# Sixteen of 62 SBUF slots begin 64 bytes later, and a planner's rule says which tiles take them

## The chip, the cores and the metric

The kernel runs on one core of a Trainium2 chip. The metric is the time of one execution on the device in microseconds (us), median of several runs.

## The reference

Two layers on a sequence of 512 tokens with 1024 features, all in float32. Each layer has a token mixer (retention in layer 0, mLSTM in layer 1) and a feed-forward part with a causal convolution. Both mixers have four heads with 256-wide queries and keys and 512-wide values. Without norms, gates and conditioning:

```
q, k, v, g = split(h @ w_in)
s   = (q @ k.T) * decay          # per head; in the mLSTM exp-weights instead of decay
y   = s @ v                      # causal, per head
x   = x + gate * ((silu(g) * norm(y)) @ w_out)
u   = conv(h2 @ w_up);  a, b = split(u)
x   = x + gate2 * ((silu(a) * b) @ w_down)
```

## The kernel before, in words

**Numbers as pairs.** Every operand of a large product is split into a high and a low part in the single-pass matmul type (names end in `h` and `l`, or are `whi` and `wlo`), and a product takes three matmuls: high by high, high by low, low by high (`mm3`, line 659). In each matmul a stationary operand, 128 by 128, is loaded by a weight load (PEld), and a moving operand of 256, 384 or 512 columns streams past it. Most weight products are folded: seven half-width products in place of eight (`PairStream`, `ValueStream`, line 781), with 256 columns each.

**Where tiles lie.** Activations lie in 62 equal slots of 128 partitions by 2048 bytes (`slot`, line 412, `NSLOTS`), weights in 18 wide tiles of 4352 bytes (`wide`, line 415). In the built program every slot begins at the same place modulo 128 bytes, and so does every wide tile. A folded weight begins `OFF` = 16 words, 64 bytes, into its wide tile (lines 552 to 640); so do the weights of the half-width contractions (`boundary`, line 1077), one block in a tile of the down projection (`Beside.low`, line 540) and the constant `ones_d`. Weights used at the full width of 512 columns have no offset.

**Attention.** `scores` (line 1293) multiplies a stretch of keys (stationary) with queries (moving) in four strips of 512, 384, 256 and 256 columns, into bank `psc`; `attend` (line 1320) multiplies values (stationary) with the weights of the scores `sh`, `sl` (moving) in the same strips, into bank `pav`. All four operands lie in slots. The pairs of values are made by `center_split` and `plain_split` (lines 1002, 1013), the keys by `rope` (line 1552, layer 0, name `qk`) and `conv_then` (layer 1, name `mqk`). Between heads stand two small products with a constant `ones_v` or `ones_1`, 512 wide: `pvar`, `pmu`, `pden`.

**The order of the work.** The kernel is first recorded as a list of calls. `Plan.run` (line 268) then plays a list scheduler over it with cost estimates and due times, and issues each engine's instructions in the order that it finds. A tile gets its slot there, when its first writer is placed: `room` holds for each kind the free slots with the time at which they come free, and the one that has been free longest is taken:

```
if b.bufs:
    b.at = room[b.key].pop(0)[1]
```

The real tile is made at issue (`Buf.get`, line 101), with a tag made of the kind and the slot number; its first writer waits for the readers of the slot's last tenant. All instructions are issued through line 387 of the kernel, so the profile's rows have that line, and names tell them apart.

Of the kernel before, what the change touches and what calls it, by code (L numbers as in the profile page):

```python
# [10 lines left out]
F32 = mybir.dt.float32  # L11
F32R = mybir.dt.float32r
# [4 lines left out]
P = 128  # L17
T = 512
# [19 lines left out]
LEAD = (4.0, 4.5)  # L38
WPAD = 64
OFF = 16  # L40
DIRECT = (0, 0)
ROOT_AT = 1
SPLIT = 4
# [3 lines left out]
NSLOTS = 62  # L47
# [46 lines left out]
class Buf:  # L94


    def __init__(self, pool, shape, dt, tag, name, bufs, psum=False):
        self.args, self.shape, self.key, self.bufs, self.psum = (pool, shape, dt, tag, name), shape, tag, bufs, psum
        self.real, self.uses, self.log, self.at = None, 0, [], ""

    def get(self):
        if self.real is None:
            pool, shape, dt, tag, name = self.args
            self.real = pool.tile(shape, dt, tag=f"{tag}{self.at}", name=name)
        return self.real

# [46 lines left out]
class Plan:  # L153
# [114 lines left out]
    def run(self):  # L268
# [38 lines left out]
        def choose(e):  # L307
# [17 lines left out]
            t, n = min((t, n) for _, n, t in cand if t > soonest)  # L325
            return t, e, n

        best = {e: choose(e) for e in engines}
        while len(out) < len(calls):
            if not any(best.values()):  # L330
# [8 lines left out]
            for b in c.bufs:  # L339
                if b.log is not None:  # L340
                    b.log, b.busy = None, 0.0
                    if b.bufs:
                        b.at = room[b.key].pop(0)[1]
                        dirty.update(engines)
                        makers[b.key].remove(b.maker)
            occ = c.occ
# [23 lines left out]
            for m, real in c.succs:  # L370
                s = calls[m]
# [19 lines left out]
def trunk(ctx: ExitStack, tc: tile.TileContext, xT, cb, pos, vec, ident, decay, zmask, ada, w_s0, w_in0, w_v0,  # L391
          w_o0, w_in1, w_v1, w_f1, w_o1, w_up, w_dn, out):
    nc = tc.nc
    const = ctx.enter_context(tc.tile_pool(name="const", bufs=1))
    slots = ctx.enter_context(tc.tile_pool(name="slots", bufs=1))
    wpool = ctx.enter_context(tc.tile_pool(name="wpool", bufs=1))
    asides = ctx.enter_context(tc.tile_pool(name="asides", bufs=1))
    cond = ctx.enter_context(tc.tile_pool(name="cond", bufs=1))
# [6 lines left out]
    def uid(s):  # L405
        count[0] += 1
        return f"{s}_{count[0]}"

    def tile_of(pool, shape, dt, tag, name):
        return Buf(pool, shape, dt, tag, name, KINDS.get(tag, 0), tag == "ps")  # L410

    def slot(s, dt=F32, w=T):
        return tile_of(slots, [P, w], dt, "s", uid(s))

    def wide(s, dt=F32):
        return tile_of(wpool, [P, WCOLS + WPAD], dt, "w", uid(s))
# [7 lines left out]
    def fixed(pool, shape, dt, name):  # L424
        b = tile_of(pool, shape, dt, name, name)
        b.get()
        return b
# [5 lines left out]


    V.memset(fixed(const, [P, 32], F32, "pad")[:], 0.0)
    ones = {}
    for name, v in (("d", 1.0 / D), ("v", 1.0 / DV), ("1", 1.0)):
        off = OFF if name == "d" else 0
# [78 lines left out]
    class Chunk:  # L517
        def __init__(self, src, n, off, added=False):
            self.off, self.added = off, added
            self.raw = wide("raw")[:, off : off + n]  # L520
            S.dma_start(self.raw, src)
# [122 lines left out]
                self.p[name] = hi, low_by(name in VADDED)(raw[r], hi, OFF)  # L644

    class Pair:
        def __init__(self, s, w=T):
            self.hi, self.lo = slot(s + "h", F32R, w), slot(s + "l", F32R, w)

        def split(self, src, r=slice(None), eng=None):  # L650
            A.copy(self.hi[:, r], src)
            (eng or V).tensor_tensor(self.lo[:, r], src, self.hi[:, r].bitcast(F32), op=ALU.subtract)

    def pair_of(s, src):
        p = Pair(s)
        p.split(src)
        return p

# [343 lines left out]
    def center_split(v, ps):  # L1002

        t, m = slot("vt"), tile_of(cols, [P, 1], F32, "vm", uid("vm"))
        tf = t[:]
        A.activation(tf, ps[:], AF.Copy, accum_out=m[:])
        G.tensor_scalar(m[:], m[:], -1.0 / DV, None, op0=ALU.mult)
        p = Pair("v")
        A.activation(p.hi[:], tf, AF.Identity, bias=m[:])
        V.scalar_tensor_tensor(p.lo[:], tf, m[:], p.hi[:].bitcast(F32), op0=ALU.add, op1=ALU.subtract)  # L1010
        v.append(p)

    def plain_split(v, ps):
        p = Pair("v")
        p.split(ps[:])
        v.append(p)

# [531 lines left out]
        A.activation(k[:], k[:], AF.Square)  # L1549
        G.tensor_scalar(cos[:], k[:], -2.0, 1.0, op0=ALU.mult, op1=ALU.add)  # L1550

    def rope(p1, p2):
        t = [slot("rp")[:] for _ in range(4)]
        V.tensor_tensor(t[0], p1[:], cos[:], op=ALU.mult)
        V.tensor_tensor(t[1], p2[:], sin[:], op=ALU.mult)
        V.tensor_tensor(t[2], p1[:], sin[:], op=ALU.mult)
        V.tensor_tensor(t[3], p2[:], cos[:], op=ALU.mult)
        V.tensor_tensor(t[0], t[0], t[1], op=ALU.subtract)
        V.tensor_tensor(t[2], t[2], t[3], op=ALU.add)
        return [pair_of("qk", t[n]) for n in (0, 2)]  # L1560

    def half_pair(st, name, finish):

        got = []

        def then(ps):
            got.append(ps)
            if len(got) == 2:
                st[name] = finish(*got)
        return then  # L1570

    h0 = []
# [262 lines left out]
    def conv_then(i, name, kt):  # L1835
        ch = (0 if name == "q" else 8) + i * 2 + kt

        def then(ps):
            acc = slot("mc")[:]
            c = lambda j: col("mcw", j * 16 + ch)  # L1840
            A.activation(acc, ps[:], AF.Identity, bias=col("mcb", ch), scale=c(3))
            for j, s in ((2, 1), (1, 2), (0, 3)):
                V.scalar_tensor_tensor(acc[:, s:], ps[:, : T - s], c(j), acc[:, s:], op0=ALU.mult, op1=ALU.add)
            A.activation(acc, acc, AF.Silu)
            M[i][name].append(pair_of("mqk", acc))
        return then

    def ml_scores(i):
# [224 lines left out]
```

## Time and profile before

| | |
|---|---|
| median of 3 runs | 1474.69 us (1473.51 to 1475.45) |
| span of the profiled execution | 1474.7 us |
| TensorE busy | 1458.4 us, 99% |
| VectorE, ScalarE, GpSimd busy | 1289.8, 1063.3, 244.5 us |

The profile shows one execution. PE is TensorE's matmuls, PEld its weight loads, DVE VectorE, ACT ScalarE, POOL GpSimd, SP the queue that issues loads. Matmuls overlap: one takes 0.28 us or more from start to end, but the next starts after 0.11 us. What a matmul costs here is therefore the step from one start to the next. It is read from the start times in the timeline, or as busy time divided by count in a stretch that holds one unbroken group of matmuls.

### The profile page before, as it was taken

The numbers are of one execution on the slowest core, as the hardware profiler recorded it, in microseconds if no ns is written. First come the engines' busy times: TensorE is split into PE (matmuls) and PEld (weight loads), VectorE is DVE, ScalarE is ACT, GpSimd is POOL, SyncE is SP. The second block draws the span as 40 slices with busy tenths as digits, with TensorE's granted clock in tenths as the row PEclk, the third lists the DMA queues.
The fourth block names the chain that finished last, engine by engine and source line by source line (L and its number), as shares of the span: only waits on it lengthen the run. The fifth ranks groups of instructions, "written<-read, shape, count | busy, mean of one in ns | idle before, by whom it ended". The sixth has DMA issues, their size and how long they took to land.

```text
span 1474.7 us, 27429 instructions
## 1 busy us (share of the span) xinstructions
PE 1458.4 (99%) x10564; PEld 1370.7 (93%) x10564; DVE 1289.8 (87%) x2183; ACT 1063.3 (72%) x1604; POOL 244.5 (17%) x279
## 2 busy tenths in 40 slices
PE   8999999999999999999999999999999999999998
PEld 7889999998999999989999998999989999999997
DVE  7899988887998888889897999999989988886866
ACT  5578768786588676666678985988856877667673
POOL 0313112112011111110001321222121011101010
PEclk8999999999999999999999999999999999999999
DMA  9868988988598999799457875888877678568661
GB/s 365 250 165 218 275 232 234 242 251 208 152 223 210 269 266 253 214 236 248 145 176 172 211 207 183 198 194 196 253 190 193 165 183 206 155 168 206 171 162 59
DMA packets 90822, 306.16 MB, mean 208 GB/s; under 512 B 11954, under 2 KB 14514, under 8 KB 90691
## 3 DMA queue, kind: packets, MB, share of 16 engines
q0 software_dynamic: 29520, 106.97, 38.6%
q1 hardware_dynamic: 60882, 197.18, 38.6%
q8 instruction: 82, 1.34, 0.4%
q10 hardware_dynamic: 288, 0.27, 0.1%
q14 instruction: 50, 0.40, 0.1%
HBM read 195.29 MB, written 2.12 MB: 134 GB/s over the span
## 4 chain that ended last, share of the span: by engine, by line
PE 49%; DMA 1%; ACT 1%; DVE 1%; issue 1%; DVEq 0%; POOL 0%; POOLq 0%
PE p L387 20%; PE po L387 16%; PE pv L387 5%; PE pf L387 3%; PE pav L387 2%; DMA wlo<-wt 1%; PE psc L387 1%; ACT whi L387 0%; PE pp L387 0%; ACT mc L387 0%; DVE sl L387 0%; DVE mc L387 0%; ACT wlo L387 0%; ACT L387 0%; DVE ws L387 0%
## 5 line engine op out<-in xcount | busy, mean ns | idle before, releaser
L387 PE MATMUL p<-hh,whi 128*128 128x256 f32 (+1 forms) x1029 | 284.7, 278 | 1.6 <-DVE p L387 1.5
L387 PE MATMUL p<-hl,whi 128*128 128x256 f32 x1024 | 283.6, 277 | 0.0
L387 PE MATMUL p<-hh,wlo 128*128 128x256 f32 x1024 | 281.6, 278 | 0.1
L387 ACT ACTIVATE wlo<-whi 128x1024 fp32r<-128x1024 f32 (+1 forms) x205 | 215.4, 1055 | 25.6 <-PE po L387 14.7
L387 PEld LDWEIGHTS p<-hh,whi 128*128 128x128 f32 x1029 | 193.9, 188 | 3.0 <-DVE p L387 2.4
L387 PEld LDWEIGHTS p<-hl,whi 128*128 128x128 f32 x1024 | 192.5, 188 | 0.4
L387 PEld LDWEIGHTS p<-hh,wlo 128*128 128x128 f32 x1024 | 191.4, 188 | 0.5 <-DMA wlo<-ws 0.3
L387 PE MATMUL p<-t24h,whi 128*128 128x256 f32 x768 | 170.4, 279 | 2.1 <-ACT fs L387 2.1
L387 PE MATMUL po<-ggl,whi 128*128 128x512 f32 (+1 forms) x448 | 153.1, 343 | 0.0
L387 PE MATMUL po<-ggh,whi 128*128 128x512 f32 (+1 forms) x448 | 152.0, 344 | 0.7 <-ACT whi L387 0.7
L387 PE MATMUL po<-ggh,wlo 128*128 128x512 f32 (+1 forms) x448 | 152.5, 343 | 0.0
L387 PE MATMUL p<-t24l,whi 128*128 128x256 f32 x512 | 142.1, 277 | 0.0
L387 DVE SCALAR_TENSOR_TENSOR x<-po,mod,x 128x512 f32<-128x512 f32 (+1 forms) x184 | 113.6, 628 | 30.7 <-PE po L387 29.8
L387 ACT CAST whi<-raw 128x1024 fp32r<-128x1024 f32 (+1 forms) x113 | 113.5, 1015 | 32.6 <-PE po L387 8.4
L387 PEld LDWEIGHTS p<-t24h,whi 128*128 128x128 f32 x768 | 130.4, 188 | 4.9 <-ACT fs L387 2.5
L387 DVE SCALAR_TENSOR_TENSOR cv<-p,vecs,cv 128x511 f32<-128x511 f32 (+1 forms) x152 | 111.2, 743 | 12.0 <-ACT cv L387 11.7
L387 DVE SCALAR_TENSOR_TENSOR ada<-ada,c_ext 128x1025 f32<-128x1025 f32 x96 | 117.6, 1227 | 0.3 <-DMA ada<-ada 0.3
L387 PE MATMUL po<-yl,whi 128*128 128x256 f32 (+1 forms) x352 | 115.3, 328 | 0.0
L387 PE MATMUL po<-yh,whi 128*128 128x256 f32 (+1 forms) x354 | 115.3, 328 | 0.0
L387 PE MATMUL po<-yh,wlo 128*128 128x256 f32 (+1 forms) x352 | 115.3, 328 | 0.0
L387 POOL DMA_DIRECT2D wlo<-wa x55 | 47.5, 864 | 366.3 <-ACT wlo L387 207.7
L387 ACT CAST whi<-ws 128x1024 fp32r<-128x1024 f32 x88 | 92.0, 1048 | 20.7 <-DVE ws L387 13.6
(292 smaller groups left out, 4394.6 us busy)
## 6 DMA issues: line engine op xcount, KB each, us to landing
ada<-ada SPq DMA_DIRECT2D x96, 512.5 KB, 6.6
wlo<-ws POOLq DMA_DIRECT2D x61, 512.0 KB, 7.6
wlo<-wa POOLq DMA_DIRECT2D x55, 512.0 KB, 6.5
wlo<-wt POOLq DMA_DIRECT2D x45, 512.0 KB, 7.5
wa<-w_up SPq DMA_DIRECT2D x38, 512.0 KB, 5.6
wb<-w_up SPq DMA_DIRECT2D x38, 512.0 KB, 8.9
wlo<-raw POOLq DMA_DIRECT2D x34, 512.0 KB, 8.2
raw<-w_o SPq DMA_DIRECT2D x32, 512.0 KB, 7.8
```

Source lines behind the costliest of these rows:

```text
L387: getattr(c.obj, c.name)(*[real(v) for v in c.a], **{key: real(v) for key, v in c.k.items()})
```

## The change

Three pools stand in place of one. The first 46 slots stay where they were. A pad of 64 bytes (`gap`) follows, then a pool of 16 slots (`shifted`, numbers 46 to 61), then a pad of 192 bytes (`gap2`); so the 16 slots begin 64 bytes later than the raster of the others, and all that lies behind them moves by 256 bytes. Two memsets on GpSimd write the pads.

A slot is no longer the one that has been free longest. A new function `place` looks at the slots that are free at the planned time. A tile that likes the shifted ones (values in both layers, keys in both layers) takes a shifted slot if one is free; a pair that does not (queries, weights of the scores, normed inputs, outputs, feed-forward products) takes a plain one if one is free; a tile without an opinion takes a shifted one while more than nine of these are free, else a plain one. Whoever finds none of its kind takes the other. Instructions are the same but for the two memsets; planned costs are the same. Since the free slots differ, so do the times at which the planner finds a slot, and the order of instructions moves in places.

```diff
+SHIFTED = 16
+SPARED = 9
+SHIFT = 16
...
     def get(self):
         if self.real is None:
             pool, shape, dt, tag, name = self.args
+            if self.shifted and self.at >= NSLOTS - SHIFTED:
+                pool = self.shifted
...
+        def place(b, t):
+
+            free_at = room[b.key]
+            if b.key != "s":
+                return free_at.pop(0)[1]
+            open_at = [i for f, i in free_at if f <= t + 1e-9]
+            shifted = [i for i in open_at if i >= NSLOTS - SHIFTED]
+            plain = [i for i in open_at if i < NSLOTS - SHIFTED]
+            if b.likes is None:
+                first = shifted if len(shifted) > SPARED else plain
+            else:
+                first = shifted if b.likes else plain
+            i = (first or shifted or plain)[0] if open_at else free_at[0][1]
+            free_at.remove(next(f for f in free_at if f[1] == i))
+            return i
...
-                        b.at = room[b.key].pop(0)[1]
+                        b.at = place(b, t)
...
+    gap = ctx.enter_context(tc.tile_pool(name="gap", bufs=1))
+    shifted = ctx.enter_context(tc.tile_pool(name="shifted", bufs=1))
+    gap2 = ctx.enter_context(tc.tile_pool(name="gap2", bufs=1))
...
-    def slot(s, dt=F32, w=T):
-        return tile_of(slots, [P, w], dt, "s", uid(s))
+    def slot(s, dt=F32, w=T, likes=None):
+        b = tile_of(slots, [P, w], dt, "s", uid(s))
+        b.likes, b.shifted = likes, shifted
+        return b
...
+    G.memset(fixed(gap, [P, SHIFT], F32, "gap_in")[:], 0.0)
+    G.memset(fixed(gap2, [P, 64 - SHIFT], F32, "gap_out")[:], 0.0)
...
     class Pair:
-        def __init__(self, s, w=T):
-            self.hi, self.lo = slot(s + "h", F32R, w), slot(s + "l", F32R, w)
+        def __init__(self, s, w=T, likes=False):
+            self.hi, self.lo = slot(s + "h", F32R, w, likes), slot(s + "l", F32R, w, likes)
...
-        p = Pair("v")
+        p = Pair("v", likes=True)
...
-        return [pair_of("qk", t[n]) for n in (0, 2)]
+        return [pair_of("qk", t[n], keys) for n in (0, 2)]
...
-            M[i][name].append(pair_of("mqk", acc))
+            M[i][name].append(pair_of("mqk", acc, name == "k"))
```

Where the order moves, two places show it. On VectorE in layer 1, at the end of the third head's work and in the middle of the fourth's projections (`p1_2107` and `p1_2123` are banks of two folded gate products, `fs_` their partial sums, `grs` the norm's root, `ada` side work on the conditioning, `mqkl` the low part of a query or key, `vl` of values, `wlo` of weights). Before:

```order
1486 L387 TENSOR_TENSOR p2_2108_12611<-p1_2107_12632,fs_2109_12636 128x256
1487 L387 TENSOR_TENSOR grs_2078_12728<-pvar_2077_12494,den_1998_12172 128x512
1488 L387 TENSOR_TENSOR whi_2122_12707<-wb_2113_12448,whi_2122_12707 128x512
1489 L387 SCALAR_TENSOR_TENSOR ada_2095_12576,mod_1_87<-ada_2095_12576,c_ext_82 128x1025
1490 L387 TENSOR_SCALAR gain_1_89<-mod_1_87,vecs_83 128x1
1491 L387 RECIPROCAL grs_2078_12728<-grs_2078_12728 128x512
1492 L387 TENSOR_TENSOR p1_2123_12715<-p1_2123_12715,fs_2125_12742 128x256
```

The same place with the change:

```order
1486 L409 TENSOR_TENSOR whi_2122_12718<-wb_2113_12454,whi_2122_12718 128x512
1487 L409 TENSOR_TENSOR mqkl_2044_12752<-mc_2042_12700,mqkh_2043_12741 128x512
1488 L409 TENSOR_TENSOR grs_2078_12761<-pvar_2077_12498,den_1998_12182 128x512
1489 L409 TENSOR_TENSOR wlo_2151_12771<-raw_2149_12629,whi_2150_12748 128x1024
1490 L409 TENSOR_TENSOR p1_2107_12635<-p1_2107_12635,fs_2109_12646 128x256
1491 L409 TENSOR_TENSOR vl_2090_12791<-pv_2073_12324,vh_2089_12765 128x512
1492 L409 RECIPROCAL grs_2078_12761<-grs_2078_12761 128x512
1493 L409 TENSOR_TENSOR p1_2123_12780<-p1_2123_12780,fs_2125_12798 128x256
```

The last add of `p1_2107`, with a low part of weights ahead of it, now stands before the reciprocal; before, it stood fifteen rows behind it. The side work on `ada_2095` has gone behind.

On TensorE, in the attention of layer 1's second head, whose folded gate products (`p2_1797`) stand between the value products (`pav`). Before:

```order
6230 L387 MATMUL pav_1802_10775<-sl_1752_10716,vh_1734_10513 128x256
6231 L387 MATMUL pav_1802_10775<-sh_1751_10695,vl_1735_10531 128x256
6232 L387 MATMUL pav_1804_10806<-sh_1741_10650,vh_1728_10443 128x512
6233 L387 MATMUL pav_1804_10806<-sl_1742_10684,vh_1728_10443 128x512
6234 L387 MATMUL pav_1804_10806<-sh_1741_10650,vl_1729_10463 128x512
6235 L387 MATMUL p2_1797_10638<-t24h_1518_9208,whi_1795_10611 128x256
6236 L387 MATMUL p2_1797_10638<-t24l_1519_9245,whi_1795_10611 128x256
```

The same place with the change:

```order
6230 L409 MATMUL pav_1802_10802<-sl_1752_10727,vh_1734_10526 128x256
6231 L409 MATMUL pav_1802_10802<-sh_1751_10707,vl_1735_10544 128x256
6232 L409 MATMUL pav_1804_10819<-sh_1741_10660,vh_1728_10456 128x512
6233 L409 MATMUL pav_1804_10819<-sl_1742_10697,vh_1728_10456 128x512
6234 L409 MATMUL p2_1797_10651<-t24h_1518_9221,whi_1795_10620 128x256
6235 L409 MATMUL p2_1797_10651<-t24l_1519_9258,whi_1795_10620 128x256
6236 L409 MATMUL p2_1797_10651<-t24h_1518_9221,whi_1795_10620 128x256
```

One of the 512-wide value products, the one with `vl_1729`, has moved behind a block of folded products; the products themselves are the same.

More of the change, by code (lines that the diff above doesn't have):

```diff
@@ L99, in __init__ @@
         self.real, self.uses, self.log, self.at = None, 0, [], ""
+        self.likes, self.shifted = None, None
     def get(self):
@@ L652, in split, with pair_of @@
             (eng or V).tensor_tensor(self.lo[:, r], src, self.hi[:, r].bitcast(F32), op=ALU.subtract)
-    def pair_of(s, src):
-        p = Pair(s)
+    def pair_of(s, src, likes=False):
+        p = Pair(s, likes=likes)
         p.split(src)
@@ L1013, in plain_split @@
     def plain_split(v, ps):
-        p = Pair("v")
+        p = Pair("v", likes=True)
         p.split(ps[:])
@@ L1550, in rope_tables, with rope @@
         G.tensor_scalar(cos[:], k[:], -2.0, 1.0, op0=ALU.mult, op1=ALU.add)
-    def rope(p1, p2):
+    def rope(p1, p2, keys):
         t = [slot("rp")[:] for _ in range(4)]
@@ L1568, in then @@
             if len(got) == 2:
-                st[name] = finish(*got)
+                st[name] = finish(*got, name == "k")
         return then
```

## Prediction

> **What bounds the kernel now.** I read the page first: the span, the busy shares, the granted clock by slices, and the chain that ended last.
>
> ```profile
> span 1474.7 us, 27429 instructions
> PE 1458.4 (99%) x10564; PEld 1370.7 (93%) x10564; DVE 1289.8 (87%) x2183; ACT 1063.3 (72%) x1604; POOL 244.5 (17%) x279
> PEclk8999999999999999999999999999999999999999
> PE 49%; DMA 1%; ACT 1%; DVE 1%; issue 1%; DVEq 0%; POOL 0%; POOLq 0%
> ```
>
> TensorE is busy for 99% of the span at full granted clock, and the chain runs through it. The view of waits, from 86 us on, says how little it waits for others:
>
> ```profile
> PE p L387 <- ACT fs L387: 2.1, 2, 1.1
> PE p L387 <- DVE p L387: 1.5, 3, 1.0
> PE po L387 <- ACT whi L387: 0.7, 1, 0.7
> PE pst L387 <- DVE rc L387: 0.6, 1, 0.6
> ```
>
> These and three smaller ones make under 6 us. So the time is the count of matmuls times their step, and I looked at whether equal matmuls have equal steps. The view of stretches, cut at the edges of unbroken groups, says no (start and end, length, PE busy with count, clock, DMA):
>
> ```profile
> 119.30:139.10 19.80, 19.78 (x168) 1.00 0.99 257
> 844.00:855.30 11.30, 11.27 (x96) 1.00 1.02 265
> 943.80:957.40 13.60, 13.57 (x120) 1.00 0.83 222
> 1020.70:1029.20 8.50, 8.47 (x72) 1.00 0.97 226
> 143.40:157.10 13.70, 13.63 (x120) 1.00 1.02 282
> 868.30:883.80 15.50, 15.50 (x132) 1.00 0.76 210
> 961.20:977.70 16.50, 16.39 (x141) 1.00 0.88 212
> 996.30:1006.30 10.00, 9.90 (x84) 1.00 0.84 203
> ```
>
> The first four are folded value products `pv`, the rest folded pair products `p`, all 256 wide. Busy by count: 117.7, 117.4, **113.1**, 117.6 ns for `pv`; **113.6**, 117.4, 116.2, 117.9 ns for `p`. There are two steps, 113.1 and about 117.6 ns, and a stretch keeps one of them for 10 or 20 us, under the same clock and with DMA shares that don't sort them. The slow ones stand behind scores, value products or the small norm products. In the timeline the entry looks so (start, duration):
>
> ```profile
> 837.87 0.28 PE L387 MATMUL p<-hh,wlo 128*128 128x256 f32 x1
> 837.98 0.28 PE L387 MATMUL pav<-sl,vh 128*128 128x256 f32 x1
> ...
> 840.93 0.28 PE L387 MATMUL pav<-sh,vh 128*128 128x256 f32 x1
> 841.05 0.28 PE L387 MATMUL pav<-sl,vh 128*128 128x256 f32 x1
> ```
>
> `p` steps by 0.11 us into the first `pav`; within `pav` the 256-wide step shown is 0.12. What differs: in `p` and `pv` the next stationary and the moving operand begin in different 64-byte halves of a 128-byte line (folded weights have the offset of 16 words, slots don't); in `pav` and `psc` both lie in slots, in the same half. Whole groups:
>
> ```profile
> 1066.00:1071.80 5.80, 5.80 (x38) 1.00 1.03 223
> 139.10:143.00 3.90, 3.88 (x24) 1.00 0.91 219
> 864.00:867.80 3.80, 3.80 (x24) 1.00 0.67 139
> ```
>
> The first holds three value tiles, 36 `pav` and two in flight at its edge: 3 x (3x512 + 3x384 + 6x256) = 12,672 columns. At 113.1/256 = 0.4418 ns a column that is 5.60 us; 5.80 are 0.20 more, **5.6 ns** a matmul. The others are `psc`, 6x512 + 6x384 + 12x256 = 8,448 columns, 3.73 us; they take 0.15 and 0.07 more, on average **4.5 ns** a matmul.
>
> **The change part by part.** *Scores and value products.* How many there are:
>
> ```profile
> L387 PE MATMUL pav<-sh,vh x128: 276/332/497, 107.6 to 1071.4; 128*128 128x256 f32 x64, 128*128 128x512 f32 x32, 128*128 128x384 f32 x32
> L387 PE MATMUL psc<-qkh,qkh x32: 278/312/402, 99.2 to 324.6; 128*128 128x256 f32 x16, 128*128 128x512 f32 x8, 128*128 128x384 f32 x8
> ```
>
> `pav` has three such groups (384), `psc` six, three in each layer (192). Extra over the fast step: 384 x 5.6 = 2.15 us, 192 x 4.5 = 0.86 us, together 3.0 us. From the slots that the planner gives in the built program: moving operand and next stationary lie in different halves for 280 of 384 `pav` (13 before) and for 147 of 192 `psc` (9 before). The rest meet because both operands got shifted slots, or both plain ones. Gain 0.73 x 2.15 + 0.77 x 0.86 = **2.2 us** if every separated one takes the fast step; bounds 0 (the address is not the cause) and 3.0 (all of it).
>
> A page of the Trainium skill speaks against this part. "TensorE: Matmul & The Clock Gate", section "Step-by-step: what each phase is for", says that the array reads weights and moving data through two independent SBUF ports, so that loading the next weights takes nothing from the running matmul; by that rule this term is 0. The two steps in the rows above don't follow from such a rule, but they don't prove the address either, since `pav` and `psc` also mix widths.
>
> *Stretches behind them.* The steps of 117.4 to 117.9 in the five slow rows cost, over 113.1: 168 x 4.6 + 96 x 4.3 + 72 x 4.5 + 132 x 4.3 + 84 x 4.8 = 2.48 us; the row at 961.20 (141, mixed) adds 3.1 x 141 = 0.44. Sum 2.9 us. If meeting operands put the matmuls into the slow step, separated ones leave them in the fast one. But the last matmul of a value product still meets the plain slot of the next stationary in the heads followed by `pv`, and the small norm products are not moved. I take half, **1.45 us**; bounds 0 and 2.9.
>
> *New meetings.* In the built program 48 half-width products of the last down projection have a feed-forward pair in a shifted slot and offset weights: 48 x 4.6 = **0.2 us** lost. If they also flip the stretch there, which now runs fast,
>
> ```profile
> 1440.00:1452.00 12.00, 12.00 (x109) 1.00 0.01 1
> ```
>
> (12.00 by 109, with two or three in flight at the edge, is about 113), the rest of that contraction, some 270 matmuls by the fast step and the 30 us that are left, loses 4.6 ns each, 1.2 us. And 64 of the full-width `po`, whose weights have no offset, get a shifted moving operand, which is worth little: 96 that meet take 21.97 us, 228.9 ns each, against 512 x 0.4418 = 226.2:
>
> ```profile
> 896.00:918.00 22.00, 21.97 (x96) 1.00 0.42 96
> ```
>
> *Reuse of slots and order.* Liked and plain tiles now draw from smaller stocks, so a slot is taken sooner after its last reader. The place with the tightest new tie is the first order shown: the copy into `fs_2125` takes the slot of `fs_2109`, whose last add moved ahead of the reciprocal.
>
> ```profile
> 1038.47 0.37 ACT L387 COPY fs<-p 128x256 f32<-128x256 f32 x1 [0.65 <-DVE grs L387]
> 1040.82 3.35 DVE L387 RECIPROCAL grs<-grs 128x512 f32<-128x512 f32 x1 [0.45 <-ACT grs L387]
> 1041.97 0.28 PE L387 MATMUL p<-t24h,whi 128*128 128x256 f32 x1
> 1051.74 1.22 DVE L387 TENSOR_TENSOR wlo<-raw,whi 128x1024 fp32r<-128x1024 f32 x1
> 1052.87 0.42 DVE L387 TENSOR_TENSOR p<-p,fs 128x256 f32<-128x256 f32 x1
> ```
>
> The copy came at 1038.47; now it waits for a low part of weights (1.22) and the add (0.42), 1.6 us later, 1040.1. The next product into that bank starts at 1041.97, so 1.5 us of cover are left: nothing, and up to a wait like those of 1.1 us above if VectorE is late there. What is queued behind the copy on ScalarE, casts of values and weights, moves with it. The one product in the second order costs its own step wherever it stands. Waits: **0**, bounds -1 and +2 us (the listed waits could also fall away).
>
> *Pads.* Two memsets on GpSimd stand ahead of its first work.
>
> ```profile
> 0.74 0.52 POOL L387 MEMSET warm<- 128x512 f32 x1 [0.29 <-POOLq L2064]
> 31.71 1.00 POOL L387 DMA_DIRECT2D wlo<-raw  x1 [30.45 <-ACT wlo L387]
> ```
>
> They are narrower than the 0.52 us of the one quoted, and 30.45 us of idling cover them. Nothing.
>
> Sum: -2.2 - 1.45 + 0.2 + 0 = -3.45; the profiled execution's 1474.7 us (the median of the runs is 1474.69) become **1471.2 us**, 0.23% less. About 0.2% (3 us) is what a measurement of this kernel can tell from no change.
>
> **The rivals.** *A, the forecast:* own range 1468.8 (both terms at their bounds, 3.0 + 2.9) to 1472.7 (2.0 alone): 0.48.
>
> *B, more goes with it.* The step is also set by waits: behind a short hitch of TensorE at 701 us, where one matmul takes 0.38 us in place of 0.28, it runs slow until 765.7.
>
> ```profile
> 701.72 0.38 PE L387 MATMUL p<-t24h,wlo 128*128 128x256 f32 x1
> ...
> 705.80:765.70 59.90, 59.90 (x511) 1.00 0.48 137
> 1094.90:1149.90 55.00, 55.00 (x485) 1.00 0.63 169
> ```
>
> The two stretches hold the same kinds of work, 117.2 against 113.4 ns each; 511 x 3.8 = 1.9 us. If all of the 2.9 us goes and a moved order spares this hitch, the time is 1474.7 - 2.2 - 2.9 + 0.2 - 1.9 = 1467.9. For: such a hitch is a matter of order. Against: nothing in the change aims at it. 0.17.
>
> *C, nothing happens.* The slow step comes from mixed widths or from the place in the stream, not from addresses; full-width `po`, equal halves, pays almost nothing, which speaks for it. Then `pav` keeps 5.6 ns, the stretches behind keep theirs, and 1474.7 + 0.2 = 1474.9. Against: fast and slow `pv` stretches have equal widths. 0.21. The Trainium skill's page named above would have it so.
>
> *D, waits take the place.* A slot taken too soon stops TensorE as at 1166 us, and the stretch behind stays slow:
>
> ```profile
> 1166.28 0.39 PE L387 MATMUL p<-hh,whi 128*128 128x256 f32 x1 [0.96 <-DVE p L387]
> 1166.50:1187.40 20.90, 20.90 (x179) 1.00 0.55 140
> ```
>
> About 1 us for the gap, and 20.90 by 179, less one in flight, is 117.4: 178 x 4.3 = 0.8; 1.8 us each. Two such stops eat the first term of the sum; with three, in layer 1's heads where the orders moved, and nothing gained behind: 1474.7 + 5.4 - 2.2 = 1477.9. For: reuse is closer. Against: TensorE's waits on such copies are only two in the whole run. 0.14.
>
> **How the numbers follow.** The likeliest is A, 1471.2. A lies around the bound of 1471.7: 0.30 of its 0.48 count as faster, 0.18 as same. B is faster. Of C, 0.19 is same and 0.02 slower; of D, 0.11 slower, 0.03 same. Faster 0.47, same 0.40, slower 0.13. The range takes in A, C and most of B, and leaves out D and B's edge: 1467.3 to 1475.3.
>
> **What would show it.** Right: three value tiles of `pav` in about 5.65 us instead of 5.80, 24 `psc` in about 3.75; `pv` and `p` stretches behind heads with a step of 113; `po` at the end still at 113. Wrong: `pav` with separated halves still at 5.80 (C); new idle time of PE behind `fs`, `vh` or `sl` (D); a fast `pav` with slow stretches behind it (the second term).

## The result, and the profile after

The change makes the kernel slower. Its median is 1479.54 us of 17 runs (1475.94 to 1483.86), against 1474.55 us of 17 runs of the kernel before (1471.38 to 1480.10): ratio 1.0034, 95% interval 1.0023 to 1.0045, or 5.0 us. Forecast were 1471.2 us.

The page of the changed kernel; this execution took 1478.88 us, 1.98 more than its span:

```profile
span 1476.9 us, 27447 instructions
PE 1460.5 (99%) x10564; PEld 1366.9 (93%) x10564; DVE 1293.1 (88%) x2183; ACT 1065.2 (72%) x1604; POOL 243.6 (16%) x281
PEclk9999999999999999999999999999999999999999
PE 47%; DVE 3%; DMA 2%; issue 1%; ACT 1%; POOL 0%; DVEq 0%; POOLq 0%; ACTq 0%
```

The same bound, the same clock, the same count of matmuls. The spans of the two traces differ by 2.2 us, less than half of what the medians differ by: one trace is one draw, and what follows leans on what several traces show alike. TensorE's waits from 86 us on (us in total, times, longest):

```profile
PE p L409 <- ACT fs L409: 2.9, 5, 1.0
PE p L409 <- DVE p L409: 1.7, 3, 1.2
PE p L409 <- DMA wlo<-wt: 0.6, 2, 0.4
PE pst L409 <- DVE rc L409: 0.6, 1, 0.6
```

Waits behind the copies `fs` grew from 2.1 us in two to 2.9 in five. Now the stretches that the prediction named, in the view of stretches (start and end, length, PE busy with count, clock, DMA): four of `pv`, two of `p`, then scores, three value tiles, the `po` of 96, and the last contraction.

```profile
118.00:137.10 19.10, 19.07 (x168) 1.00 1.00 261
840.00:851.30 11.30, 11.26 (x96) 1.00 1.03 248
940.00:953.60 13.60, 13.59 (x120) 1.00 0.79 215
1018.00:1026.50 8.50, 8.50 (x72) 1.00 0.96 226
...
141.40:155.00 13.60, 13.60 (x120) 1.00 0.99 255
914.70:931.10 16.40, 16.40 (x145) 1.00 0.79 201
...
137.10:140.90 3.80, 3.80 (x24) 1.00 0.99 224
860.00:863.80 3.80, 3.80 (x24) 1.00 0.65 121
...
1064.00:1069.90 5.90, 5.90 (x38) 1.00 0.88 203
...
892.00:914.20 22.20, 22.16 (x96) 1.00 0.40 95
1440.00:1452.00 12.00, 12.00 (x107) 1.00 0.00 1
```

`pv` steps are 113.5, 117.3, 113.3 and 118.1 ns: one of four became fast, none slow. Scores save a tenth of a us in one of two groups. Three value tiles take 5.90 us, not the 5.65 that were expected (5.80 before). This sign tests less than it was meant to: in the built program 37 of that head's 48 value products still read both operands from the same half, since its values got plain slots. `po` with some moving operands in late slots takes 230.8 ns in place of 228.9, and the last contraction passes 107 products in 12 us, where 109 passed.

To add this up I take the step from each matmul's start to the next, less 0.4427 ns for each column (113.3 ns for 256, 226.7 for 512), from 86 us on; steps more than 25 ns over that are counted apart, as stalls. The sums of the excess, in us, for the kernel before, the changed one, and three of the experiments below:

| tile | before | changed | changed, slots unshifted | old order, late by rule | old order, late settled |
|---|---|---|---|---|---|
| `pav` and `psc` | 3.10 | 2.58 | 3.16 | 2.42 | 2.47 |
| `pv` | 2.41 | 1.96 | 2.49 | 1.77 | 2.22 |
| `p` and `pf` | 7.02 | 5.76 | 4.69 | 5.70 | 6.49 |
| `po` | 3.80 | 4.54 | 2.54 | 5.88 | 2.92 |
| stalls, all tiles | 15.0 | 18.3 | 18.3 | 12.9 | 14.2 |

Each column is one trace, and one stretch in it can go either way. Behind 703 us the 511 products of the stretch that rival B named (59.90 us before) take, in the changed kernel and in the one with the old order and late slots by the rule:

```profile
703.80:761.70 57.90, 57.89 (x511) 1.00 0.49 141
...
702.30:762.10 59.80, 59.80 (x510) 1.00 0.49 140
```

That is 2 us between the fast and the slow step, at `po` and `pf` alike, with the same places. The traces of f2 and e2 below have the same order and differ here (57.90 and 59.80), and the second has no stall in front of it. So neither the order nor a hitch decides it; what does stays open. Of the excess of `p`, `pf` and `po` together, 2.2 us before and in the old order with late slots by the rule come from this stretch.

**Two new losses show in the trace.** The first lies in the second feed-forward layer. There blocks of 12 `po` alternate with 72 and 12 `p`, evenly over 200 us. These are unbroken stretches of 72 `p`, ahead of the blocks from 1308 to 1361 us, in them, at their end, and behind them:

```profile
1299.70:1307.90 8.20, 8.20 (x72) 1.00 0.54 194
1314.80:1323.30 8.50, 8.50 (x72) 1.00 0.83 182
...
1361.00:1369.50 8.50, 8.48 (x72) 1.00 0.85 216
1376.40:1384.50 8.10, 8.10 (x72) 1.00 0.58 155
```

From 113.9 to 118.1 ns, and back to 112.5 (the windows end on tenths of a us; by starts the slow ones are 4.45 ns over the fast step). In the built program one tile tells these blocks from the rest: the low part of one feed-forward product, `ggl_2610`, lies in a late slot. It is the moving operand of one full-width `po` in each of eight blocks, while the next stationary, a `wlo` with the offset of folded weights, begins in the same half: one meeting, in the eleventh matmul of twelve. What comes behind it stays in the slow step until a block without that tile. Four of the eight are followed by 72 `p` and four by 12, at 4.45 ns over the fast step: 336 x 4.45 = 1.5 us.

The second lies in the fourth head of layer 1. The timeline of TensorE before (start, duration), with the second group of twelve into a bank at its end:

```profile
1036.64 0.28 PE L387 MATMUL p<-t3h,wlo 128*128 128x256 f32 x1
1036.76 0.28 PE L387 MATMUL p<-hh,whi 128*128 128x256 f32 x1
...
1037.89 0.28 PE L387 MATMUL p<-hh,wlo 128*128 128x256 f32 x1
1038.00 0.28 PE L387 MATMUL p<-t24h,whi 128*128 128x256 f32 x1
```

and with the change, TensorE and what it waits for:

```profile
1032.93 1.53 DVE L409 SCALAR_TENSOR_TENSOR mc<-p,vecs,mc 128x511 f32<-128x511 f32 x2
...
1033.40 0.28 PE L409 MATMUL p<-t3h,wlo 128*128 128x256 f32 x1
1033.71 0.37 ACT L409 COPY fs<-p 128x256 f32<-128x256 f32 x1 [0.31 <-PE p L409]
...
1034.38 0.42 DVE L409 TENSOR_TENSOR p<-p,fs 128x256 f32<-128x256 f32 x1
...
1034.86 0.38 PE L409 MATMUL p<-t24h,whi 128*128 128x256 f32 x1 [1.19 <-DVE p L409]
```

In the order of TensorE, bank `p2_2108` got 12 products, then 11 of two other banks (`p1_2123`, `p2_2124`) came, then its next 12; now its 24 stand in a row. Between the two groups the bank must be copied and added. The 11 products covered that; now TensorE waits for the copy and for the add, which stands behind two steps of a convolution (`mc`) on VectorE.

### The profile page after: what moved, and what is told of

Same layout as the page of the kernel before. It is cut to its first block, busy times and chain, and to the rows that moved or that the text cites. A ratio compares the mean times of both kernels' runs of the same rounds, so it can differ in the third digit from the quotient of the medians.

```text
span 1476.9 us, 27447 instructions
## 1 busy us (share of the span) xinstructions
PE 1460.5 (99%) x10564; PEld 1366.9 (93%) x10564; DVE 1293.1 (88%) x2183; ACT 1065.2 (72%) x1604; POOL 243.6 (16%) x281
## 4 chain that ended last, share of the span: by engine, by line
PE 47%; DVE 3%; DMA 2%; issue 1%; ACT 1%; POOL 0%; DVEq 0%; POOLq 0%; ACTq 0%
PE p L409 21%; PE po L409 15%; PE pv L409 5%; PE pf L409 3%; PE pav L409 2%; DMA wlo<-wt 1%; PE psc L409 1%; PE pp L409 0%; DVE x L409 0%; DMA mb<-scratch 0%; DVE cv L409 0%; POOL zv L409 0%; DVE ada L409 0%; DVE xr L409 0%; ACT whi L409 0%
## 5 line engine op out<-in xcount | busy, mean ns | idle before, releaser
L409 ACT ACTIVATE wlo<-whi 128x1024 fp32r<-128x1024 f32 (+1 forms) x205 | 215.5, 1056 | 26.6 <-PE po L409 15.5
L409 DVE SCALAR_TENSOR_TENSOR x<-po,mod,x 128x512 f32<-128x512 f32 (+1 forms) x184 | 113.1, 626 | 26.6 <-PE po L409 26.0
L409 DVE SCALAR_TENSOR_TENSOR ada<-ada,c_ext 128x1025 f32<-128x1025 f32 x96 | 118.3, 1234 | 0.4 <-DMA ada<-ada 0.4
```

The source lines that it names most:

```text
L409: getattr(c.obj, c.name)(*[real(v) for v in c.a], **{key: real(v) for key, v in c.k.items()})
```

## The experiments

Eighteen kernels were run. "Order" is that in which the planner issues; "reuse" which tile follows which in a slot; "late" slots are the 16 (or 14, 12) that begin later. Ratios are to the kernel before on the same chip, with 95% intervals. First the six kernels that settle the question (old order and new, by what slots are late):

| | old order | new order |
|---|---|---|
| none late, new reuse | 1.0002 (0.9991 to 1.0012) | 1.0017 (1.0006 to 1.0029) |
| late, settled after planning | 0.9999 (0.9987 to 1.0011) | 1.0016 (1.0007 to 1.0025) |
| late, by the rule of the change | 1.0019 (1.0005 to 1.0032) | 1.0034 (1.0023 to 1.0045) |

The order costs 0.15 to 0.17% in each row, late slots by the rule 0.17% in each column, against none late. Neighbouring intervals touch; the pattern rests on six runs that agree.

### Order, reuse, late slots

**e1_after_128** and **e3_reuse_alone**. The first is the changed kernel with

```diff
-SHIFT = 16
+SHIFT = 32
```

> The changed kernel with the eighteen... that is, its sixteen late slots beginning 128 bytes later instead of 64, so that no slot begins in the other half of a 128-byte line: the order of all instructions, the choice of slots and so the reuse of slots are those of the changed kernel, the halves are those of the kernel before. Theory 1 (the moved order and the closer reuse cost: the matmuls' stalls over 20 ns grew from 27.6 to 31.0 us, and what the halves gave, 1.4 us, was not enough): 1479 to 1482 us, as slow as the changed kernel or slower. Theory 2 (the halves cost: full-width output products with a late slot as moving operand and the folded stretches behind them take the slow step, so that shifted addresses lose as much as they gain): 1474 to 1475.5 us, like the kernel before. In between, 1476 to 1478: both.

1483.58 us, ratio 1.0053 (1.0034 to 1.0073). The second has the old order as well (its edit is that of the next kernel):

> The order of the kernel before and the slots of the preference rule, with the late slots 128 bytes later instead of 64, so that no half changes: against the kernel before, only which tile follows which in a slot differs. The median time from the end of a slot's last use to its next first use, by the planner's times, falls from 21 to 13 us, and the reuses closer than 1 us rise from 75 to 108. Theory 1a (closer reuse itself makes engines wait): the run with the changed order and no halves lost 9 us against the kernel before, the run with the old order and the halves 3.4; if halves give 4 us in this order too, this one comes to 1481 to 1483 us. Theory 1b (the moved order alone makes the loss, reuse is free): 1474 to 1476 us.

1480.68 us, 1.0027 (1.0017 to 1.0038). Taken at their word, both put the whole loss on order and reuse. They were not the neutral controls that I thought: a later kernel showed that places 128 bytes on matter too. The unshifted kernels further down replace them.

**e2_order_before.** The planner keeps its old list; a second list gives the place.

```diff
+        here = list(room["s"])
...
-            free_at = room[b.key]
+            b.turn_at = room[b.key].pop(0)[1]
             if b.key != "s":
-                return free_at.pop(0)[1]
+                return b.turn_at
+            free_at = here
...
```

> The shifted slots with the order of the kernel before: the scheduler plans with its old list of free slots, so that no instruction moves, and a second list gives the tile its slot by the preferences of the change. Late slots begin 64 bytes later, as in the change. Theory 1 (moved order and closer reuse cost, halves gain 1.4 to 2.2 us): 1472.3 to 1473.5 us if it is the moved order, up to 1476 if the closer reuse, which this kernel keeps, has a part in it. Theory 2 (halves cost): about 1479 us, like the changed kernel.

1477.99 us, 1.0019 (1.0005 to 1.0032): slower than before without any moved instruction, between the two theories' numbers and nearer to the second. Late slots and reuse cost something by themselves.

**e7_order_alone.** The mirror image: the planner takes places by the rule, the tile gets the slot free longest, still with 128 bytes.

```diff
-                        b.at = place(b, t)
+                        b.at = b.turn_at = place(b, t)
+                        if b.key == "s":
+                            b.at = here.pop(0)[1]
...
```

> The order of the changed kernel, all instructions of TensorE, VectorE, ScalarE and SyncE in its sequence, but each tile takes the slot that has been free longest, as before the change, and the late slots begin 128 bytes later, so that no half changes. Theory 1b (moved order costs): 1481 to 1484 us, like the run with the changed order and reuse and no halves (1483.6). Theory 1a (closer reuse costs): 1474 to 1476 us.

1493.98 us, 1.0121 (1.0106 to 1.0137), far outside both. The stalls in its trace are shorter than those in the changed kernel's (15.5 and 18.3 us from 86 us on, against 15.0 before), but the excess of its steps is 32.9 us (15.1 and 16.6). Here normed inputs lie 128 bytes on too, while folded weights lie 64 on, and of the 1533 `p` of that kind 98% are in the slow step. The order was not to blame; my control was.

**f1_after_unshifted, f2_reuse_alone, f3_order_alone.** The same three without any late slot:

```diff
-        b.likes, b.shifted = likes, shifted
+        b.likes = likes
...
-    G.memset(fixed(gap, [P, SHIFT], F32, "gap_in")[:], 0.0)
-    G.memset(fixed(gap2, [P, 64 - SHIFT], F32, "gap_out")[:], 0.0)
```

> The changed kernel with all its slots at their old places, none later by any bytes and without the two pads: its order of instructions and its reuse of slots alone. It replaces the run with 128 bytes, which was no neutral control: in the run with the changed order and slots in turn, products with the moving operand 128 bytes on and the weights 64 bytes on were slow in 98% of their steps, so places count modulo 256 bytes (quarters of 64), not 128. Theory 1 (order and reuse cost): 1479 to 1482 us. Theory 2 (places cost: it was the 16 late slots that made full-width output products and the stretches behind them slow): 1474 to 1476 us.

> The kernel before, instruction by instruction and with the same 62 slots, but tiles take their slot by the preference rule: only which tile follows which is changed. If closer reuse costs: 1478 to 1481 us, like the run with 128 bytes in this order (1480.7). If that run was slow because of its places 128 bytes on: 1474 to 1476 us, like the kernel before.

> The order of the changed kernel with slots taken in turn and at their old places: the moved order alone. If the order costs: 1478 us or more. If the 18 us that this order lost with 16 slots 128 bytes on came from those places (its slow step had 33 us in all, 16.6 in the kernel before, and its stalls were no longer): 1474 to 1477 us.

1478.29 us, 1.0017 (1.0006 to 1.0029); 1476.20, 1.0002 (0.9991 to 1.0012); 1478.72, 1.0018 (1.0007 to 1.0029). Closer reuse costs nothing that can be measured; the moved order costs about 2.5 us, with the old reuse or the new. The blocks of the second feed-forward layer run fast in the unshifted kernel (`p`, in the same place as the slow one above):

```profile
1314.90:1323.00 8.10, 8.10 (x72) 1.00 0.84 182
```

**h2a_order_second, h2b_order_first.** Unshifted, with the rule in one half of the planned time:

```diff
-            if b.key != "s":
+            if b.key != "s" or t < 690.0:
```

(`t >= 690.0` in the second).

> All slots at their old places; up to 690 us of planned time tiles take the slot that has been free longest, from then on by the preference rule, so that only the second layer pair is planned in a new order (the whole at unshifted places: 1478.3, ratio 1.0017). If the cost lies there, as the traces of the changed order say (stalls of TensorE between 690 and 1115 us 6.1, 6.5, 5.7 and 5.6 us in four runs with it, 2.8 to 3.8 in five runs with the old order): 1477.5 to 1479 us. If it is spread over the program or lies in the first half: 1475 to 1476.5 us.

> The counterpart: the preference rule up to 690 us of planned time, the old rule from then on, all slots at their old places. If the cost lies in the second half: 1475 to 1476 us, like the kernel before. If in the first: 1477.5 to 1479 us.

1476.41 us, 1.0007 (0.9997 to 1.0017), and 1476.16, 1.0006 (0.9994 to 1.0018). Neither answers clearly: the cost is not all in one half. The waits of TensorE between 950 and 1052 us do answer for their place. The second-half order has

```profile
PE p L409 <- DVE p L409: 1.0, 1, 1.0
PE p L409 <- ACT fs L409: 0.5, 1, 0.5
```

and the first-half order only

```profile
PE p L409 <- DVE p L409: 0.2, 1, 0.2
```

These two waits, of 1.0 to 1.2 us at 1034 us and 0.5 at 962, stand in the traces of the changed kernel, of f1, of f3, of h2a and of h3, and not in those of the kernel before, of e2, of f2 or of h2b. The second has the same cause: `p2_1965` now gets 24 products in a row where 12 and 12 were parted by 12 of another bank. Together they are some 1.6 us of the order's 2.5; where the rest lies stayed open. Nor is their price sure: by the medians h2a, which has both, lost 1.0 us, and h2b, which has neither, 0.8, and both intervals take in no loss at all.

**e6_settled, e6_settled_128, h3_after_settled.** Slots given after planning, when lives are known: `likes` are settled first (a tile still takes the other kind where none of its own is free), tiles without an opinion go to the side with more room.

```diff
...
+        for b in start:
+            if b.likes is not None:
+                put(b, int(b.likes))
+        for b in sorted((b for b in start if b.likes is None), key=lambda b: start[b] - end.get(b, 1480.0)):
+            put(b, int(np.argmax([size[s] - load[s, span(b)].max() for s in (0, 1)])))
...
```

> A candidate: the order of the kernel before; slots are given after the planning, when each tile's life is known: keys and values go to 14 late slots (64 bytes later), the other matmul operands to the rest, and the tiles that are no operands to the side with more room over their life, each in the slot that has been free longest. The spread of the times between uses of a slot stays that of the kernel before at the close end (78 closer than 1 us, 75 before; 108 by the rule of the change), 305 of 384 value products that step on to another read from different halves as wanted, and of the full-width output products only 16 have the late slot as moving operand (72 in the changed kernel). If reuse is the cost and halves give 2 to 4 us: 1471 to 1473 us, faster than both kernels. If halves give nothing with the old order: 1474 to 1475.5 us.

> The candidate with its 14 late slots 128 bytes later, so that no half changes: only the other choice of slots is left, with the spread of reuse of the kernel before. If close reuse is the cost: 1474 to 1475.5 us, like the kernel before. If any new choice of slots costs (by where in memory tiles come to lie): 1477 to 1482 us.

1475.50 us, 0.9999 (0.9987 to 1.0011); 1475.82, 0.9998 (0.9987 to 1.0009). With the old order and no feed-forward tile late the loss is gone, but no gain can be measured either: 325 of 384 value products apart instead of 280 (the expectation's 305 was a miscount), and the time of the kernel before. The same in the new order:

> The changed kernel with its own order and its 16 late slots, but slots are given after the planning, when each tile's life is known, so that no tile of the feed-forward layers' output products lies late and 8 full-width output products in all have a late moving operand (72 in the changed kernel); keys and values are in late slots at least as often (92 of 96 value products of 384 columns apart, 72 in the changed kernel). If the late slots' half of the loss is the misplaced operands: 1476.5 to 1478 us, at most what the order alone takes (1478.7). If late keys and values themselves cost: 1479.5 us, like the changed kernel.

1477.86 us, 1.0016 (1.0007 to 1.0025): the order's cost alone. The late slots' half goes when the misplaced operands go.

### What the places do

**e4_all_meet.** The kernel before with

```diff
-OFF = 16
+OFF = 32
```

> The kernel before with the folded weights' offset of 32 words instead of 16, so that they begin in the same half of a 128-byte line as the slots: the order is unchanged, and of some 8100 matmuls of 256 columns whose two operands lie in different halves none is left. If the halves set the step (113.1 against 117.6 ns), and the kernel before has 16 us of the slow step's excess in it: 8100 x 4.5 = 36 us in place of 16, so 1490 to 1500 us. If the halves have nothing to do with the step (two read ports that do not meet): 1474.5 us, within 1 us.

1509.41 us, 1.0226 (1.0206 to 1.0246), 33 to 35 us more, beyond the 15 to 25 expected. There is a third step. Stretches of `pv` and of the 72 `p`:

```profile
859.20:870.90 11.70, 11.66 (x96) 1.00 1.05 274
...
1372.40:1381.10 8.70, 8.66 (x72) 1.00 0.68 146
```

120 to 122 ns, or by starts 113.3 + 6.6. Of the some 5350 `p`, 91% are slow here, 6.0 ns over on average; before it was 24% and 1.1. In this kernel the two operands of a folded product lie in the same half of 128 bytes, but two quarters of 256 bytes apart (slots at 0, weights at 128); that the second counts is shown by the next two kernels. The place sets the step: rival C's premise, that addresses are not the cause, is gone.

**e5_swapped** and **g1_swapped_next.** All slots 64 bytes later in both; folded weights at 0, or at 128.

```diff
-OFF = 16
+OFF = 0
...
+    gap = ctx.enter_context(tc.tile_pool(name="gap", bufs=1))
     slots = ctx.enter_context(tc.tile_pool(name="slots", bufs=1))
...
+    G.memset(fixed(gap, [P, 16], F32, "gap_in")[:], 0.0)
...
```

> The kernel before with the halves exchanged: all slots begin 64 bytes later and the folded weights at 0. Matmuls of 256 columns read from different halves as before, with the sides exchanged; scores and value products still read from one half; but some 1250 full-width output products and 300 other full-width products that read both operands from the first half now have the moving operand in the second and the stationary in the first. Theory 2 (a full-width product whose moving operand is in the second half and whose stationary is in the first is slow: the changed kernel's trace has 3.2 to 4.6 ns more for each in two of three such groups): 1550 x 3.5 = 5 us more, 1479 to 1481 us, and the folded products after them begin in the slow step. Theory 1 (halves of full-width products are worth nothing): 1474 to 1475.5 us.

> As the run with exchanged places (all slots 64 bytes later, folded weights at 0: 1496.5 us), but the folded weights lie 128 bytes behind the line, so that they are again one quarter of 256 bytes behind the slots. Modulo 128 bytes nothing differs from that run. If only halves of 128 bytes count: 1495 to 1498 us. If quarters count, and the stationary operand one quarter behind the moving one is the fast place: the 7000 pair and output products of 256 columns go back from 3 to 4.4 ns over the fast step to about 1.2, so 15 to 20 us less, 1477 to 1482 us.

1496.53 us, 1.0135 (1.0112 to 1.0158), and 1488.59, 1.0095 (1.0079 to 1.0112). The first is 16 us above what theory 2 said, since nearly all the fold of the second feed-forward layer is slow, not only the full-width products. With the weights at 0, `p` at 142.6 and `pv` at 119.2 us:

```profile
142.60:156.70 14.10, 14.10 (x120) 1.00 1.02 271
...
119.20:138.20 19.00, 19.00 (x168) 1.00 1.00 263
```

With the weights at 128, the same two stretches:

```profile
143.90:157.60 13.70, 13.70 (x120) 1.00 1.05 297
...
119.70:139.60 19.90, 19.88 (x168) 1.00 1.00 259
```

117.5 and 113.1 ns became 114.2 and 118.3: they changed places. Modulo 128 bytes the two kernels are one, so the raster is not 128. The time fell by 8 us, not by the 15 to 20 expected: the fold of the second feed-forward layer stayed slow (8.50 us for 72), behind full-width `po` that read from different quarters in both.

**f4_values_192** and **g2_settled_values_192.** Folded weights of values 192 bytes on instead of 64, in the kernel before and in the settled one.

```diff
+VOFF = 48
...
-                raw[name] = wide("wv")[:, OFF : OFF + WCOLS]
+                raw[name] = wide("wv")[:, VOFF : VOFF + WCOLS]
```

> The kernel before, its order and slots unchanged; the folded weights of values alone lie 192 bytes behind the line instead of 64 (their tiles have 256 bytes of room), so that in the products of folded values the stationary operand (a slot) lies one quarter of 256 bytes behind the moving one, as in the folded pair products, and not three. If quarters count, and one quarter on is the fast place: the 1000 products of 256 columns fall from 2.4 ns over the fast step to the 1.1 of the pair products, 1.3 us, and stretches behind them follow: 1471.5 to 1473.5 us. If only halves of 128 bytes count (192 and 64 are then the same place): 1474.5 to 1475.5 us, no change.

> The two parts that lost nothing or gained, together: the order of the kernel before, keys and values settled in 14 late slots after the planning, and the folded weights of values at 192 bytes. If the gains add up: 1474.6 - 0.1 - 2.2, that is 1472 to 1474 us, faster than both kernels. If settled slots cost where values are at 192: 1474.5 to 1476 us.

1473.96 us, 0.9985 (0.9973 to 0.9997), the only kernel faster than both; and 1475.61, 1.0002 (0.9993 to 1.0011). In the traces `pv` fell to 1.51 us of excess in the first (2.41 before), and not in the second (2.53). The gain of 0.15% did not repeat in the second, so it stays unsure.

**h1_outputs_late.** The settled kernel in the old order, with 12 late slots for the feed-forward's moving operands instead of keys and values.

```diff
+            likes = s == "gg"
```

> The order of the kernel before, with 12 late slots settled for the tiles gg, the moving operands of the feed-forward's output products; keys and values are not put there. 453 full-width output products then have a late moving operand and a stationary one at 0 (64 in the changed kernel), 115 are the last of a block and meet the next folded weights in the same place (8 in the changed kernel), and 447 of the last 1152 of 256 columns meet (48). If a block that ends with such a meeting leaves the folded products behind it in the slow step, as the changed kernel's trace shows for its four blocks from 1308 to 1361 us: some 2000 folded products x 4.4 ns = 8.7 us, 447 x 4.4 = 2 us, and 0.7 us for the full-width ones, so 1483 to 1490 us. If the meeting costs only itself: 562 x 4.4 = 2.5 us, 1476 to 1478 us.

1486.51 us, 1.0078 (1.0065 to 1.0092): 11 us, as a block that leaves the products behind it slow would have it, four times the 2.5 us estimated for the meetings by themselves. The 72 `p` behind a block that meets, and behind one of the last blocks:

```profile
1368.60:1377.00 8.40, 8.40 (x72) 1.00 0.87 205
1384.00:1392.20 8.20, 8.18 (x72) 1.00 0.64 154
```

By starts they are 4.47 and 0.36 ns over the fast step.

## Why the prediction was wrong

3.5 us less were forecast, 5.0 more came. Two terms that the sum put at nothing or next to it, the order (0) and the new meetings (+0.2), cost about 2.5 and 2.3 us, and the two gains came only in part.

- **That places set the step: right, and incomplete.** e4 and the pair e5 and g1 show it. There are three steps (113.3, 117.8 and 119.9 ns for 256 columns), not two, and the raster is not 128 bytes.
- **Scores and value products, -2.2 us: failed.** "If every separated one takes the fast step" did not hold. `pav` and `psc` together kept 2.58 of 3.10 us, so 0.5 us went; 2.42 to 2.58 in the five kernels with keys and values 64 bytes late (the changed one, e2, e6, h3, g2). Separated `psc` of 256 columns fell to 2.0 ns (5.7 before for those that meet), but separated ones of 384 and 512 columns stay near 5, and `pav` at 4.0 (256) and 5.2 to 5.9 (384, 512): these keep the slow step. Rival C's mixed widths may be what holds them; no run has strips of one width, so that is not shown.
- **Stretches behind them, -1.45 us: seen in layer 0 only.** Up to 400 us, in the first layer's attention, `pv` and `p` have 1.5 and 2.1 us of excess in the two kernels with late slots by the rule, 2.6 and 2.7 in e6 and h3, and 3.4 to 3.9 in the six with none late and weights in their old places (before, f1, f2, f3, h2a, h2b). In layer 1 the traces show no such gain. Over the whole run `pv` lost 0.45 us of excess and `p` with `pf` 1.3 in this trace, but the unshifted kernel of the same order lost 2.3 in `p` and `pf` with no late slot at all: the trace of before that I sized this term from was on the slow side, in the stretch behind 703 us among others.
- **Full-width `po`, "worth little", and the new meetings, +0.2 us: failed, the largest loss of the late slots.** I priced a meeting at its own 4.6 ns and looked for flipped stretches only behind the 48 half-width ones. The eight full-width ones in the fold cost 1.5 us through the 336 `p` behind them. In the second feed-forward layer, from 1210 us on, the excess is 3.42 us; it is 1.13 in the kernel before, in f1, f2 and e6, 1.14 in h3 and 1.19 in f3, and again 3.42 in e2. That is 2.3 us: 1.5 in those `p`, some 0.2 in eight other `po` blocks with a late operand, and 0.5 in the last contraction. There the 48 cost 11 ns each, not 4.6: they come in threes, each three puts about seven products into the slow step, and then the stream is fast again, so the flip of 1.2 us did not come. Another 0.6 us went to full-width `po` of layer 0 with late operands. The settled kernels, with late keys and values but without these, cost 2.7 to 3.0 us less than the rule's. Against none late the rule costs 2.5 us, the balance of such losses and of the gains above; one trace of each kernel does not close it to the us.
- **Reuse and order, 0 within -1 and +2 us: failed on the order, right on reuse.** The order costs 2.5 us, half of the loss and a little outside my bounds (1.6 us of it seen as waits, the rest not located); the place that I checked (the copy into `fs_2125` at 1038.47 us) stood half a us behind the product that came to wait (1038.00). I compared the order of VectorE there and missed that TensorE's two groups into `p2_2108` had closed up.
- **Rival B's** hitch did not decide: its stretch ran fast in the changed kernel's trace, 2 us less, and the time rose all the same.
- **Rival D** had the right sign and part of the cause, waits that take the place. Its price came from three stops of 1.8 us; two stops of 1.6 us in all were found, and late slots did the rest.
- **Pads: nothing**, as said; no run isolates them, but e6, which has them, loses nothing.

## What to carry to other kernels

When equal instructions have two durations, ask what puts a stretch into the slow one, and price a trigger by the stretch behind it, not by itself: here one tile in the wrong place made 336 products slow. A change of a planner's resource list is a change of order; look on the engine that sets the time for groups into one bank that have closed up, since what stood between them was cover. And a control must be neutral in the thing tested: a shift thought to have no effect misled three runs, where no shift at all gave the answer.

## What the runs showed of the hardware

- A 256-wide matmul's step is 113.3, about 117.8 or about 119.9 ns at full granted clock, by where its moving operand and the next stationary begin in SBUF and by what went ahead. In quarters of 256 bytes (moving, stationary), mean excess of the folded products: (0, 2) 6.0 ns in e4, (0, 1) 1.1 before, (1, 0) 2.4 before (`pv`) and 3.1 in e5 (`p`), (1, 2) 2.2 in g1, (2, 1) 3.5 in g1 and 4.7 in e7. The 24 to 98% of slow steps behind these means come in stretches, so they mix the place with what went ahead. Which pairs can be fast, why the same pair (0, 1) runs fast in one trace and slow in another behind 703 us, and whether 256 is the whole raster, is not settled.
- The slow step holds on: a single meeting at full width put 12 or 72 products with good places into it, in eight blocks of the changed kernel's trace and the same eight of e2's. It does not always hold: behind each of the 16 groups of three in the last contraction it was over within four products. The Trainium skill, "TensorE: Matmul & The Clock Gate", section "Step-by-step: what each phase is for", has weights and moving data come through two independent ports, so that loading the next weights takes nothing from the running matmul. e4, with the same instructions in the same order at other addresses and 33 to 35 us more, does not fit that rule, but no run shows what the two operands share.
- The time varies by up to 9 us between executions of one kernel (1471.38 to 1480.10 us for the kernel before), while the fold of the second feed-forward layer repeats to 0.1 us of excess. Long, regular stretches are the place to read small effects.
